# A post-norm decoder step on one core: the decode chain's tiles per step, its key products and the pace of its steps

## The chip, the cores and the metric

One core of a Trainium2 chip runs the whole program. The metric is the device time of one execution in microseconds, the median of the runs; lower is better. Engines are called as the profile calls them: PE (TensorE matmul), PEld (its weight load), DVE (VectorE), ACT (ScalarE), POOL (GpSimd), SP (SyncE, which here issues the prompt's DMAs).

## The reference, cut to what matters

One decoder layer is applied to two groups of requests that share all weights: a prompt of 1024 tokens, and eight requests that each decode one token against 4096 cached tokens.

```python
def trunk_layer(x, ...):                       # D_MODEL 1024, D_FF 2816, float32
    x = layer_norm(ALPHA * x + 0.5 * swiglu(x, f1_in, f1_out), ...)       # first half step
    h = x @ w_mix_in                                                       # q, k, v, u, vb: 5 x 512
    oa = diff_head_out(attend(q, k, v, lam), subln_g, lambda_init)         # 4 heads, 2 x 64 wide
    ob, vn = causal_sgu(u, vb, ...)
    x = layer_norm(ALPHA * x + concatenate([oa, ob]) @ w_mix_out, ...)
    x = layer_norm(ALPHA * x + cross_attn(x, mk, mv, xq_w, xo_w), ...)
    x = layer_norm(ALPHA * x + 0.5 * swiglu(x, f2_in, f2_out), ...)        # second half step

def sample_attend(ck, cv, page_table, table):  # the decode group's attend
    k_past = ck[page_table]; v_past = cv[page_table]      # 8 requests x 32 pages x 128 rows x 512
    ... softmax(q k_past / 8 + bias), two halves, p0 - lam * p1, times v_past
```

## The kernel before, in words

The prompt's work fills PE. Its matmuls have 344 (or 336) columns and come in threes, since each float32 operand is split into a high and a low part (`proj`, lines 150 to 152; the half step's `out`, lines 628 to 630). `ffn` walks eleven groups of two hidden blocks over three chunks of tokens; `unit` loads a block of weights by SP, and ACT and DVE split it (lines 63, 64). Line 635 adds a group's output to the accumulator on DVE. Then come `mix_first` and `mix_in` (projections of q, k, v and the gating unit), `attention`, `cross` and the second `ffn`.

The decode group's work is a generator, `decode`, which the prompt's loops advance. `beat(cols)` adds `rate[dstage] * cols / 8192` to a credit, and each whole credit runs one step of the chain (`step_dec`). So a rate is steps per 8192 matmul columns of the prompt, called a unit below. Stage 0 is the chain's own first half step and projection, stage 1 the key products, stage 2 the values. A scheduler in the compiler orders each engine's instructions by a timeline of its own; in stage 0, and in attention from its fifth step on, a step's instructions are held behind the PE matmul before it, in stage 1 behind a DVE instruction. In the other parts of stage 2 they can be moved earlier.

- **Stage 0** (`decode_keys`, lines 338 to 418, and `decode_sgu`): POOL loads one tile of weights a step into one of four buffers (`dec_stage`, line 332), and PE multiplies it by the eight tokens in four column groups of 32: 64 tiles of `w_in` (line 363), 32 of `w_out` (line 380), 24 of `w_mix_in` (line 406). Rate 2.6.
- **Stage 1** (lines 441 to 461): 17 tiles for each of eight requests; 16 of them are gathered from the paged cache by an indirect DMA on POOL (line 448), two rows of 512 a partition. DVE multiplies the tile by the query `qb` (line 453), and reduces the first row (line 454); ACT reduces the second row with eight accumulating copies (line 458). Lines 463 to 490 then make the softmax. Rate 1.0. When `ffn`'s last group begins, `before()` runs what is left (`dec_until(2)`).
- **Stage 2** (`decode_values`): one gathered tile a step (line 550), eight matmuls of one weight column on it (line 554). Its rate is 0 up to `mix_in`, there 0.9, 1.0, 4.0 and 0 for the four heads (line 835), and 2.0 in `attention` (line 1040). The scores `sc` lie in the pool of the four buffers; the pool `dv2` is opened in `before()` (line 1443).

From the code's own arithmetic, a group of `ffn` gives 18 units, `mix_first` 21, `mix_in` 43.5 and attention some 40. With the rates before, stage 0 ends in the third group, the key steps run to the tenth, `mix_in` issues 53 of the 128 value steps and attention 75.

Of the kernel before, what the change touches and what calls it, by code (L numbers as in the profile page):

```python
# [8 lines left out]
F32 = mybir.dt.float32  # L9
# [23 lines left out]
class Trunk:  # L33
    def __init__(self, ctx, tc, a, stop=None):
        self.ctx, self.tc, self.nc, self.a = ctx, tc, tc.nc, a
        self.stop = stop
        self.bg, self.free = [], []
        self.pinned = False
# [284 lines left out]
    def decode(self):  # L323
        with ExitStack() as ck:
            yield from self.decode_keys(self.pool("dk", 1, ck, side="right"))
        self.dstage = 2
        yield
        yield from self.decode_values()
        self.dstage = 3

    def dec_stage(self):
        return self.dv.tile([P, D], F32, tag="stg", bufs=4, name="stg")

    def decode_keys(self, dk):
# [19 lines left out]
        gT = dk.tile([P, 8, P], F32, name="gT")  # L354
        for s in range(4):
            ps = self.dec_bank()
            for half in range(2):
                c0 = half * D_FF + s * 704
                for k in range(KT):
                    st = self.dec_stage()  # L360
                    q.dma_start(st[:, :704], w_in[k * P:(k + 1) * P, c0:c0 + 704])
                    for j in range(4):
                        mm(ps[32 * j:32 * j + 32, half * 256:half * 256 + 176], xT[:, k], st[:, j * 176:(j + 1) * 176],
                           start=(k == 0), stop=(k == KT - 1))
                    yield
            t = dk.tile([P, 176], F32, tag="dt", bufs=1, name="dt")
            nc.scalar.activation(t, ps[:, :176], AF.Silu)
            nc.vector.tensor_tensor(t, t, ps[:, 256:432], op=ALU.mult)
            yield
            ps = self.dec_bank()  # L370
            for hh in range(2):
                nc.tensor.transpose(ps[:88, hh * P:(hh + 1) * P], t[:, hh * 88:(hh + 1) * 88], self.ident)
            nc.vector.tensor_copy(gT[:88, 2 * s:2 * s + 2], ps[:88, :256].rearrange("p (h i) -> p h i", h=2))
        ps = self.dec_bank()
        for n in range(32):
            s, j, hh = n // 8, n % 8 // 2, n % 2
            st = self.dec_stage()
            q.dma_start(st[:88], w_out[n * 88:(n + 1) * 88, :])
            for jj in range(4):
                mm(ps[32 * jj:32 * jj + 32, :256], gT[:88, 2 * s + hh, 32 * j:32 * j + 32],  # L380
                   st[:88, jj * 256:(jj + 1) * 256], start=(n == 0), stop=(n == 31))
            yield
# [15 lines left out]
        for g in range(3):  # L398
            ns = 2 if g < 2 else 1
            ps = self.dec_bank()  # L400
            for k in range(KT):
                st = self.dec_stage()
                q.dma_start(st[:, :512 * ns], w[k * P:(k + 1) * P, g * 1024:g * 1024 + 512 * ns])
                sv = st[:, :512 * ns].rearrange("p (s j c) -> p s j c", s=ns, j=4)
                for j in range(4):
                    mm(ps[32 * j:32 * j + 32, :P * ns], xT[:, k], sv[:, :, j], start=(k == 0), stop=(k == KT - 1))
# [11 lines left out]
        yield from self.decode_sgu(dk)  # L418

# [116 lines left out]
    def decode_values(self):  # L536
# [5 lines left out]
        for s in range(ND):  # L542
# [5 lines left out]
            for rr in range(16):  # L548
                st = self.dec_stage()
                q.indirect_dma_start(out=st, out_offset=None, in_=pages,  # L550
                                     in_offset=bass.IndirectOffsetOnAxis(ap=self.idx[:, s, rr:rr + 1], axis=0))
                for r in range(2):
                    for h in range(4):
                        mm(ps[32 * h:32 * h + 1, cs], self.sc[:, s, 2 * rr + r, 2 * h:2 * h + 1],  # L554
                           st[:, r * 512 + h * P:r * 512 + (h + 1) * P], start=(rr + r == 0), stop=False,
                           tile_position=(0, 32 * h))
                yield
# [239 lines left out]
    def mix_in(self, XH, XL, sl, tok):  # L797
# [36 lines left out]
        for h in range(4):  # L834
            self.rate[2] = (0.9, 1.0, 4.0, 0.0)[h]
# [77 lines left out]
    def attention(self, aq, at):  # L913
# [114 lines left out]
        for x in range(n + 4):  # L1028
# [9 lines left out]
            if x == 4:  # L1038
                self.pinned = True
                self.rate[2] = 2.0  # L1040
# [328 lines left out]
    def run(self):  # L1369
# [17 lines left out]
        self.sc = self.dv.tile([P, ND, 33, 8], F32, name="sc")  # L1387
        if self.stop == "dec":
            self.dec = self.decode()
            self.dec_until(2)  # L1390
            self.dv2 = self.pool("dv2", 1, cd, side="right", reuse_waits="tile")
# [7 lines left out]
        with ExitStack() as cx:  # L1399
# [5 lines left out]
            with ExitStack() as c1:  # L1405
# [35 lines left out]
                def before():  # L1441
                    self.dec_until(2)
                    self.dv2 = self.pool("dv2", 1, cd, side="right", reuse_waits="tile")
# [109 lines left out]
```

## Time and profile before

| | |
|---|---|
| median of 3 runs | 2597.42 us (2595.98 to 2598.25) |
| the profiled execution's own time | 2591.04 us |
| its span, first to last instruction | 2589.3 us |
| PE busy | 2476.6 us, 96% |
| DVE, ACT, POOL busy | 54%, 35%, 16% |
| mean granted clock of PE | 0.979 of full speed |

Busy PE is not PE at its peak: matmuls are pipelined, and one that waits for the one ahead counts as busy. What a stretch of PE's timeline costs is read from start to start. A granted clock below 1.00 in a stretch means that for part of it PE ran at the lower of its two levels, 1.2 instead of 2.4 GHz.

### The profile page before, as it was taken

The numbers are of one execution on the slowest core, as the hardware profiler recorded it, in microseconds if no ns is written. First come the engines' busy times: TensorE is split into PE (matmuls) and PEld (weight loads), VectorE is DVE, ScalarE is ACT, GpSimd is POOL, SyncE is SP. The second block draws the span as 40 slices with busy tenths as digits, with TensorE's granted clock in tenths as the row PEclk, the third lists the DMA queues.
The fourth block names the chain that finished last, engine by engine and source line by source line (L and its number), as shares of the span: only waits on it lengthen the run. The fifth ranks groups of instructions, "written<-read, shape, count | busy, mean of one in ns | idle before, by whom it ended". The sixth has DMA issues, their size and how long they took to land.

```text
span 2589.3 us, 45161 instructions
## 1 busy us (share of the span) xinstructions
PE 2476.6 (96%) x18032; PEld 2339.5 (90%) x18032; DVE 1387.4 (54%) x2706; ACT 908.5 (35%) x3334; POOL 422.3 (16%) x510
## 2 busy tenths in 40 slices
PE   8999999999999899898899999799999999999997
PEld 6777899999999799888677899789999999999997
DVE  4323388777778745614665473746633333333337
ACT  3111176666665341214655142533411111111110
POOL 2221243323332202120334000111000000000000
PEclk9999999999999899999999999999999999999999
DMA  6766566656654538778999732732211111111101
GB/s 214 233 199 185 188 200 203 187 181 194 192 184 142 198 124 267 249 238 260 272 301 311 248 110 96 231 108 75 66 50 49 49 42 47 43 50 49 50 17 66
DMA packets 294362, 399.28 MB, mean 154 GB/s; under 512 B 17132, under 2 KB 230948, under 8 KB 294152
## 3 DMA queue, kind: packets, MB, share of 16 engines
q0 software_dynamic: 57632, 205.00, 24.6%
q1 hardware_dynamic: 236520, 191.40, 24.4%
q8 instruction: 141, 2.31, 0.4%
q14 instruction: 69, 0.57, 0.1%
HBM read 352.68 MB, written 45.25 MB: 154 GB/s over the span
## 4 chain that ended last, share of the span: by engine, by line
PE 69%; DMA 9%; issue 6%; DVE 3%; ACT 1%; POOL 1%; SPq 0%; POOLq 0%; ACTq 0%; DVEq 0%
PE mm L150 16%; PE mm L151 16%; PE mm L152 16%; PE mm L628 5%; PE mm L629 5%; PE mm L630 5%; DMA stg<-cache_v,idx 4%; PE dec L554 1%; DMA raw<-xkv_w 1%; DMA stg<-cache_k,idx 1%; DVE stg L453 1%; DMA xqb<-xrows 1%; DMA qb<-rows 1%; PE dx L993 0%; DVE xst L1261 0%
## 5 line engine op out<-in xcount | busy, mean ns | idle before, releaser
L150 PE MATMUL mm<-XH,wh 128*128 128x344 f32 (+1 forms) x1536 | 497.8, 325 | 5.7 <-ACT XH L63 5.4
L152 PE MATMUL mm<-XH,wl 128*128 128x344 f32 (+1 forms) x1536 | 492.6, 321 | 0.0
L151 PE MATMUL mm<-XL,wh 128*128 128x344 f32 (+1 forms) x1536 | 492.3, 321 | 0.0
L63 ACT CAST wh<-raw 128x1024 fp32r<-128x1024 f32 x192 | 198.7, 1048 | 592.0 <-PE mm L629 274.6
L150 PE MATMUL mm<-YH,wh 128*128 128x344 f32 x1216 | 390.3, 321 | 6.0 <-ACT wh L63 6.0
L151 PE MATMUL mm<-YL,wh 128*128 128x344 f32 x1216 | 389.6, 320 | 0.0
L152 PE MATMUL mm<-YH,wl 128*128 128x344 f32 x1216 | 389.1, 320 | 0.0
L628 PE MATMUL mm<-gh,wh 128*128 128x344 f32 (+1 forms) x1040 | 336.3, 325 | 10.2 <-DVE g L611 5.0
L64 DVE TENSOR_TENSOR wl<-raw,wh 128x1024 fp32r<-128x1024 f32 x192 | 233.4, 1222 | 209.1 <-ACT wh L63 205.9
L629 PE MATMUL mm<-gl,wh 128*128 128x344 f32 (+1 forms) x1040 | 335.4, 323 | 0.0
L630 PE MATMUL mm<-gh,wl 128*128 128x344 f32 (+1 forms) x1040 | 334.6, 322 | 0.0
L150 PEld LDWEIGHTS mm<-XH,wh 128*128 128x128 f32 x1536 | 290.8, 190 | 18.2 <-issue 11.4
L152 PEld LDWEIGHTS mm<-XH,wl 128*128 128x128 f32 x1536 | 290.0, 189 | 5.5 <-issue 5.4
L151 PEld LDWEIGHTS mm<-XL,wh 128*128 128x128 f32 x1536 | 290.1, 189 | 4.9 <-issue 4.5
L458 ACT ACTIVATE stg<-stg 128x64 f32<-128x64 f32 x1024 | 246.7, 243 | 111.9 <-DVE stg L453 72.7
L611 DVE TENSOR_TENSOR g<-g,mm 128x344 f32<-128x344 f32 (+1 forms) x132 | 67.2, 509 | 347.7 <-PE mm L152 345.8
L150 PEld LDWEIGHTS mm<-YH,wh 128*128 128x128 f32 x1216 | 228.8, 188 | 8.6 <-ACT wh L63 6.8
L151 PEld LDWEIGHTS mm<-YL,wh 128*128 128x128 f32 x1216 | 228.9, 188 | 0.5 <-issue 0.4
L152 PEld LDWEIGHTS mm<-YH,wl 128*128 128x128 f32 x1216 | 228.7, 188 | 0.1
L628 PEld LDWEIGHTS mm<-gh,wh 128*128 128x128 f32 x1040 | 196.8, 190 | 19.6 <-issue 6.1
L550 POOL DMA_INDIRECT stg<-cache_v,idx x128 | 131.8, 1029 | 472.4 <-PE dec L554 429.9
L448 POOL DMA_INDIRECT stg<-cache_k,idx x128 | 157.5, 1230 | 284.1 <-DVE sc L454 119.4
(421 smaller groups left out, 4166.4 us busy)
## 6 DMA issues: line engine op xcount, KB each, us to landing
raw<-ffn_w_in SPq DMA_DIRECT2D x88, 512.0 KB
stg<-ffn_w_in POOLq DMA_DIRECT2D x64, 352.0 KB
raw<-ffn_w_out SPq DMA_DIRECT2D x44, 512.0 KB
stg<-ffn_w_out POOLq DMA_DIRECT2D x32, 352.0 KB
raw<-w_mix_in SPq DMA_DIRECT2D x20, 512.0 KB
stg<-w_mix_in POOLq DMA_DIRECT2D x16, 512.0 KB
raw<-xkv_w SPq DMA_DIRECT2D x16, 512.0 KB
xst<-cache_mem_k POOLq DMA_DIRECT2D x16, 512.0 KB
```

The costliest lines, as they stand in the source:

```text
L63: self.nc.scalar.copy(hi, src)
L64: self.nc.vector.tensor_tensor(lo, src, hi.bitcast(F32), op=ALU.subtract)
L150: mm(ps, wh[:, ks], xh[:, k], start=(i == 0), stop=False)
L151: mm(ps, wh[:, ks], xl[:, k], start=False, stop=False)
L152: self.pe_last = mm(ps, wl[:, ks], xh[:, k], start=False, stop=(i == KT - 1))
L448: q.indirect_dma_start(out=st, out_offset=None, in_=pages, in_offset=bass.IndirectOffsetOnAxis(ap=self.idx[:, s, rr:rr + 1], axis=0))
L458: nc.scalar.activation(v, v, AF.Copy, accum_out=sc[:, s, 2 * rr + 1, x:x + 1])
L550: q.indirect_dma_start(out=st, out_offset=None, in_=pages, in_offset=bass.IndirectOffsetOnAxis(ap=self.idx[:, s, rr:rr + 1], axis=0))
L611: self.anchor = nc.vector.tensor_tensor(g, g, pb, op=ALU.mult)
L628: nc.tensor.matmul(ps, wh[:, ds], gh, start=(i == 0), stop=False)
L629: nc.tensor.matmul(ps, wh[:, ds], gl, start=False, stop=False)
L630: self.pe_last = nc.tensor.matmul(ps, wl[:, ds], gh, start=False, stop=(i == len(fs) - 1))
```

## The change

Stage 0 collects four tiles and issues their matmuls in one step; its rate becomes 0.8 and its buffers seven (three more in the pool `dk`). The key stage gets pools of its own, so `sc` and the key buffers are allocated after stage 0. Of a key tile's product, DVE makes the first row and POOL the second; of the second row's reduction DVE takes four of the eight sums and ACT the other four; the query tile has two buffers; the rate becomes 1.3. A value step takes two tiles; its rate is 0.65 from the moment that the key stage ends, 0.4 in `mix_in` and 0.3 in attention. By the same arithmetic the key steps now end in the ninth group of `ffn`; the value tiles fall so: 50 in `ffn`, 28 in `mix_first`, 36 in `mix_in`, 14 in attention.

```diff
-        self.rate = [2.6, 1.0, 0.0, 0.0]
+        self.rate = [0.8, 1.3, 0.65, 0.0]
...
     def decode(self):
         with ExitStack() as ck:
-            yield from self.decode_keys(self.pool("dk", 1, ck, side="right"))
+            dk = self.pool("dk", 1, ck, side="right")
+            self.extra = [(dk, 3), (self.dv, 4)]
+            yield from self.decode_inputs(dk)
+            self.extra = []
+        self.sc = self.pool("dsc", 1, self.cd, side="right", reuse_waits="tile").tile([P, ND, 33, 8], F32, name="sc")
+        with ExitStack() as ck:
+            yield from self.decode_keys(self.pool("dk2", 1, ck, side="right", reuse_waits="tile"))
+        self.dv2 = self.pool("dv2", 1, self.cd, side="right", reuse_waits="tile")
         self.dstage = 2
...
     def dec_stage(self):
-        return self.dv.tile([P, D], F32, tag="stg", bufs=4, name="stg")
-
-    def decode_keys(self, dk):
+        pool, n = (self.dv, 4)
+        if self.extra:
+            self.staged = (self.staged + 1) % sum(n for _, n in self.extra)
+            pool, n = self.extra[0] if self.staged < self.extra[0][1] else self.extra[1]
+        return pool.tile([P, D], F32, tag="stg", bufs=n, name="stg")
+
+    def decode_inputs(self, dk):
...
                     q.dma_start(st[:, :704], w_in[k * P:(k + 1) * P, c0:c0 + 704])
-                    for j in range(4):
-                        mm(ps[32 * j:32 * j + 32, half * 256:half * 256 + 176], xT[:, k], st[:, j * 176:(j + 1) * 176],
-                           start=(k == 0), stop=(k == KT - 1))
+                    sts.append((half, k, st))
+                    if len(sts) < 4:
+                        continue
+                    for half, k, st in sts:
+                        for j in range(4):
+                            mm(ps[32 * j:32 * j + 32, half * 256:half * 256 + 176], xT[:, k],
+                               st[:, j * 176:(j + 1) * 176], start=(k == 0), stop=(k == KT - 1))
+                    sts = []
                     yield
...
-            qb = dk.tile([P, 512], F32, tag="qb", bufs=1, name="qb")
+            qb = dk.tile([P, 512], F32, tag="qb", bufs=2, name="qb")
...
-                nc.vector.tensor_tensor(sv, sv, qb.unsqueeze(1).to_broadcast([P, nr, 512]), op=ALU.mult)
+                nc.vector.tensor_tensor(sv[:, 0], sv[:, 0], qb, op=ALU.mult)
+                if nr == 2:
+                    q.tensor_tensor(sv[:, 1], sv[:, 1], qb, op=ALU.mult)
                 nc.vector.tensor_reduce(sc[:, s, 2 * rr], sv[:, 0].rearrange("p (x d) -> p x d", d=64), axis=AX.X, op=ALU.add)
                 if nr == 2:
-                    for x in range(8):
+                    nc.vector.tensor_reduce(sc[:, s, 2 * rr + 1, 4:], sv[:, 1, 256:].rearrange("p (x d) -> p x d", d=64),
+                                            axis=AX.X, op=ALU.add)
+                    for x in range(4):
...
-            for rr in range(16):
-                st = self.dec_stage()
...
+            for r0 in range(0, 16, 2):
+                sts = []
+                for rr in (r0, r0 + 1):
+                    st = self.dec_stage()
+                    q.indirect_dma_start(out=st, out_offset=None, in_=pages,
+                                         in_offset=bass.IndirectOffsetOnAxis(ap=self.idx[:, s, rr:rr + 1], axis=0))
+                    sts.append((rr, st))
+                for rr, st in sts:
...
-            self.rate[2] = (0.9, 1.0, 4.0, 0.0)[h]
+            self.rate[2] = 0.4
...
-                self.rate[2] = 2.0
+                self.rate[2] = 0.3
```

`w_out` and `w_mix_in` are collected by four in the same way. `dv2` is no longer opened in `before()`.

## Rows read from the trace of the kernel before

**Rows 1.** Busy time by stage: stretch, length, engines' busy us (instructions), granted clock, DMA share, GB/s
```profile
20.00:310.00 290.00, 282.96 (x2283) 226.08 (x2284) 93.86 (x188) 49.93 (x87) 67.60 (x126) 0.98 0.65 200
...
370.00:840.00 470.00, 468.05 (x2987) 466.55 (x2987) 378.88 (x551) 302.72 (x1933) 150.59 (x130) 1.00 0.60 185
...
985.00:1190.00 205.00, 193.04 (x1733) 181.91 (x1730) 91.23 (x182) 46.65 (x75) 41.12 (x45) 0.98 0.79 251
1190.00:1270.00 80.00, 64.40 (x583) 54.95 (x581) 42.77 (x113) 42.85 (x122) 15.80 (x17) 0.91 1.03 295
1270.00:1446.00 176.00, 164.00 (x1908) 133.36 (x1908) 101.29 (x306) 93.47 (x285) 64.15 (x70) 0.97 0.92 293
```
**Rows 2.** Timeline of PE, weight steps alone and four together: start, us, engine, line
```profile
103.95 0.32 PE L630 MATMUL mm<-gh,wl 128*128 128x344 f32 x1
104.20 0.51 PE L363 MATMUL dec<-stg,xT 128*32 128x176 f32 x8
104.64 0.42 PE L628 MATMUL mm<-gh,wh 128*128 128x344 f32 x1
...
113.37 1.40 PE L363 MATMUL dec<-stg,xT 128*32 128x176 f32 x32
114.70 0.42 PE L629 MATMUL mm<-gl,wh 128*128 128x344 f32 x1
```
**Rows 3.** Busy time of VectorE's product line L453 alone in the key stage
```profile
370.00:840.00 470.00, 140.32 (x121) 1.00 0.60 185
```
**Rows 4.** Busy time of VectorE's reduction line L454 alone in the key stage
```profile
370.00:840.00 470.00, 79.24 (x121) 1.00 0.60 185
```
**Rows 5.** Groups of VectorE by line and shape, 330 to 815 us
```profile
L453 DVE TENSOR_TENSOR stg<-stg,qb 128x1024 f32<-128x1024 f32 x126 | 151.6, 1220 | 39.3 <-DMA stg<-cache_k,idx 23.7 <-DMA qb<-rows 14.2 <-issue 1.3
...
L453 DVE TENSOR_TENSOR stg<-stg,qb 128x512 f32<-128x512 f32 x8 | 5.5, 687 | 0.0
```
**Rows 6.** Timeline of POOL and of VectorE in the key stage
```profile
503.33 0.93 POOL L448 DMA_INDIRECT stg<-cache_k,idx  x1 [6.00 <-DVE g L611]
509.68 1.59 POOL L448 DMA_INDIRECT stg<-cache_k,idx  x1 [5.41 <-DVE A L635]
...
509.24 1.22 DVE L453 TENSOR_TENSOR stg<-stg,qb 128x1024 f32<-128x1024 f32 x1
```
**Rows 7.** Groups of POOL by line: one with data of 128 elements a partition
```profile
L723 POOL TENSOR_SCALAR_AFFINE_SELECT sgw<-sgw 128x128 f32<-128x128 f32 x4 | 1.0, 312 | 0.0
```
**Rows 8.** Timeline of PE, value steps alone and two together
```profile
1146.10 0.62 PE L554 MATMUL dec<-stg,sc 128*1 128x128 f32 x16
1146.64 0.43 PE L152 MATMUL mm<-XH,wl 128*128 128x336 f32 x1
...
1136.80 1.06 PE L554 MATMUL dec<-stg,sc 128*1 128x128 f32 x32
1137.78 0.42 PE L151 MATMUL mm<-XL,wh 128*128 128x344 f32 x1
```
**Rows 9.** Busy time of the value line L554 alone, by stretch
```profile
840.00:900.00 60.00, 12.88 (x240) 5.76 (x240) 0.89 0.60 200
...
985.00:1190.00 205.00, 21.03 (x592) 13.63 (x592) 0.98 0.79 251
1190.00:1446.00 256.00, 48.26 (x1200) 24.52 (x1200) 0.95 0.96 294
```
**Rows 10.** Chain of waits in attention, 1190 to 1446 us, by line
```profile
by line: DMA stg<-cache_v,idx 25.1%; DMA raw<-xkv_w 13.6%; PE dec L554 8.1%; issue 6.4%; PE dx L993 5.0%; PE mm L150 4.9%; PE mm L151 4.9%; PE mm L152 4.7%; DMA q<-scr_qh 4.2%; PE f L985 3.4%; PE s L955 3.4%; PE s L960 2.6%; DMA kh<-scr_kh 
```
**Rows 11.** A wait of PE in attention: us in total, times, longest
```profile
PE dec L554 <- DMA stg<-cache_v,idx: 9.1, 9, 3.7
```
**Rows 12.** Chain of waits behind attention: start us, us, what
```profile
1450.24 2.14 DMA OLs<-dol
1452.61 1.05 ACT wh L63
1453.70 0.65 PE mm L150
```

More of the change, by code (lines that the diff above doesn't have):

```diff
@@ L37, in __init__ @@
         self.bg, self.free = [], []
+        self.extra, self.staged = [], 0
         self.pinned = False
         self.dec, self.dstage, self.credit, self.anchor, self.pe_last = None, 0, 0.0, None, None
-        self.rate = [2.6, 1.0, 0.0, 0.0]
+        self.rate = [0.8, 1.3, 0.65, 0.0]
         self.cst = self.pool("cst", 1)
@@ L378, in decode_keys @@
             q.dma_start(st[:88], w_out[n * 88:(n + 1) * 88, :])
-            for jj in range(4):
-                mm(ps[32 * jj:32 * jj + 32, :256], gT[:88, 2 * s + hh, 32 * j:32 * j + 32],
-                   st[:88, jj * 256:(jj + 1) * 256], start=(n == 0), stop=(n == 31))
+            sts.append((n, gT[:88, 2 * s + hh, 32 * j:32 * j + 32], st))
+            if len(sts) < 4:
+                continue
+            for n, g, st in sts:
+                for jj in range(4):
+                    mm(ps[32 * jj:32 * jj + 32, :256], g, st[:88, jj * 256:(jj + 1) * 256], start=(n == 0), stop=(n == 31))
+            sts = []
             yield
@@ L403, in decode_keys @@
                 q.dma_start(st[:, :512 * ns], w[k * P:(k + 1) * P, g * 1024:g * 1024 + 512 * ns])
-                sv = st[:, :512 * ns].rearrange("p (s j c) -> p s j c", s=ns, j=4)
-                for j in range(4):
-                    mm(ps[32 * j:32 * j + 32, :P * ns], xT[:, k], sv[:, :, j], start=(k == 0), stop=(k == KT - 1))
+                sts.append((k, st[:, :512 * ns].rearrange("p (s j c) -> p s j c", s=ns, j=4)))
+                if len(sts) < 4:
+                    continue
+                for k, sv in sts:
+                    for j in range(4):
+                        mm(ps[32 * j:32 * j + 32, :P * ns], xT[:, k], sv[:, :, j], start=(k == 0), stop=(k == KT - 1))
+                sts = []
                 yield
@@ L418, in decode_keys @@
         yield from self.decode_sgu(dk)
+    def decode_keys(self, dk):
+        nc, a = self.nc, self.a
+        mm = nc.tensor.matmul
+        q = nc.gpsimd
         pt = dk.tile([P, ND], I32, name="pt")
@@ L547, in decode_values @@
             q.dma_start(vn, self.rows[2, s:s + 1, :])
-            for rr in range(16):
-                st = self.dec_stage()
[L550 to L556, printed above, removed]
+            for r0 in range(0, 16, 2):
+                sts = []
+                for rr in (r0, r0 + 1):
[4 more added lines that the diff above has]
+                for rr, st in sts:
+                    for r in range(2):
+                        for h in range(4):
+                            mm(ps[32 * h:32 * h + 1, cs], self.sc[:, s, 2 * rr + r, 2 * h:2 * h + 1],
+                               st[:, r * 512 + h * P:r * 512 + (h + 1) * P], start=(rr + r == 0), stop=False,
+                               tile_position=(0, 32 * h))
                 yield
@@ L1386, in run @@
         self.dv = self.pool("dv", 1, cd, side="right")
-        self.sc = self.dv.tile([P, ND, 33, 8], F32, name="sc")
+        self.cd = cd
         if self.stop == "dec":
@@ L1390, in run @@
             self.dec_until(2)
-            self.dv2 = self.pool("dv2", 1, cd, side="right", reuse_waits="tile")
             self.dec_until(3)
@@ L1442, in before @@
                     self.dec_until(2)
-                    self.dv2 = self.pool("dv2", 1, cd, side="right", reuse_waits="tile")
                     lnp.append(self.pool("lnp", 1, c1, side="right", reuse_waits="tile"))
```

## The prediction

> **What bounds the kernel now.** I read the busy times by stage first [rows 1]. In the key stage, 370 to 840 us, PE is dense: 468 of 470 us, clock 1.00, and 2987 matmuls give 0.157 us each from start to start. A unit of 8192 columns is 24 such matmuls, about 3.8 us. DVE is busy 379 of the 470 us there, so PE is the bound and DVE stands close behind. Around it PE is not dense. In stage 0 it also carries the chain's small matmuls. In attention it is idle for 15.6 us of the 80 up to 1270 us and for 12.0 of the 176 behind, at granted clocks of 0.91 and 0.97 (what is missing there is time at 1.2 GHz), while the DMA engines are full (shares of 1.03 and 0.92). The chain of waits in attention names the value tiles' loads first, 25.1% of 256 us [rows 10], and PE itself waited 9.1 us for such tiles [rows 11]. So the chain costs twice: as small matmuls between the large ones, and as loads that attention waits for.
>
> **The change, part by part.** *Stage 0.* A w_in step alone takes PE from the 103.95 us matmul to the 104.64 us one: 0.69 us, less the 0.16 of the large matmul, so 0.53. Four steps that the scheduler happened to put together take 1.33 us from their own start to the next large matmul, with the same lead-in of 0.25 us, less 0.16: 1.42 [rows 2]. So each border between the two kinds of matmul costs (4 x 0.53 - 1.42) / 3 = 0.23 us, whatever lies between. I counted the timeline's runs: 96 for the 120 tiles, two of which stand in the rows. The change makes 30. 66 borders at 0.23 give **-15 us**, all on PE's path. What it adds: the fourth tile of a step can load only when the step before has given its buffers back, and four DMAs then stand behind one another on POOL, which is busy for 68 of 290 us there [rows 1], so its queue has room. A step comes every 1.25 units, 4.7 us and its own 1.4. No row shows a late tile's price; the bounds are no wait at all and 0.5 us in each of the 30 steps, 15 us, which would give the gain back. I take no wait, since the DMA share is 0.65.
>
> *Query tile.* DVE sat idle 14.2 us for eight query loads [rows 5]; PE felt little of it, being within 2 us of dense [rows 1]. A second buffer takes **-2**; bounds 0 and -5.
>
> *Key stage.* A tile costs DVE 140.32 / 121 = 1.16 us for the product [rows 3] and 79.24 / 121 = 0.65 for the reduction [rows 4]; the other 159 us of its 379, over some 124 units, are the prompt's, 1.29 us a unit. At 1.3 tiles a unit a tile has 2.92 us, of which 0.99 are the prompt's. The product of one row is 687/1220 of the whole [rows 5], 0.65; the reduction stays 0.65; half a row more is by the same ratio 0.37. Together 2.66 of 2.92: **0.26 us a tile to spare**. POOL gets a product that no row shows. Its nearest rows are DVE's 0.69 us for the same data [rows 5] and POOL's 0.312 us for a quarter of the elements with one input [rows 7], times four 1.25; I take 1.0. With 0.93 to 1.59 us for a gather [rows 6] POOL then has 1.9 to 2.6 us of work in 2.92. On POOL the product waits for its tile, and later gathers queue behind it; four buffers leave room for three of them. DVE's added reduction waits for POOL's product, with the prompt's weight splits queued behind it, and PE waits for those.
>
> The row at 509.68 us shows what the two engines do to each other: a gather that takes 0.93 us beside no product takes 1.59 beside DVE's product of 509.24, ending 0.8 us behind it, while that product keeps its 1.22 us [rows 6]. So POOL gave way. Whether DVE gives way to a POOL product no row shows: the bounds are 0 and the whole product, 1.25 us a tile. I take 0.36, a third of 1.0 as the chance to meet, and little more: 0.10 beyond the spare for 136 tiles, **+14 us**. The Trainium skill (SBUF — State Buffer, section Who interferes with whom) speaks against this edit: a DVE instruction with two SBUF inputs and a GpSimd instruction that reads SBUF take a shared read interface, and the later one waits for the whole of the other. The trace agrees as far as the gather that stretched to 1.59 us. The skill (GPSIMD Engine Reference, section 3.1 Elementwise) also gives 4497 ns for a two-input operation on 2048 elements, by estimate 1.1 us here; by that price and the same third the term would be +19 instead of +14.
>
> ACT loses four of its eight copies a tile; nothing waits for ACT there, so that is nothing. The softmax of the scores moves from the last group of the half step into the ninth; it is DVE work among dense PE either way: nothing, with 0 to -5 for the norm behind the half step, which then starts on a freer DVE.
>
> *Values.* A step alone costs 0.25 + 0.54 - 0.16 = 0.63 us of PE, two together 0.25 + 0.98 - 0.16 = 1.07 [rows 8]. 64 pairs for 128 steps: 68.5 instead of 80.6, -12. Some stand together already (+3). And 240 of the records, 15 steps, lie in the norm's hole at 840 to 900 us, 12.9 us [rows 9], where PE has nothing else; a hole now filled only by half gives back some 5. Left: **-4**. This holds the moves: of 75 steps in attention 14 tiles stay, the other 61 cost the half step and the projections 61 x 0.54 = 33 us and attention gets back 61 x 0.64 = 39 [rows 9].
>
> *What attention waits for.* Idle time 27.6 us; at clocks of 0.91 and 0.97 the lower level fills some 25 us, of which half, 12, is lost [rows 1]: 40 in all. 61 of 75 tiles leave, and their loads are the first name on the chain [rows 10]; other names (xkv_w 13.6%, q 4.2%) waited in part because of them. I take 60%, **-24**; bounds 0 and -40. Late next is xkv_w.
>
> *The chain's tail.* Behind attention PE stood until 1453.70 us for ACT's split of 1452.61, which waited for the chain's last DMA [rows 12]. The tail now runs inside attention: **-8**, the 6 us hole and some of the slower matmuls behind it; bounds -5 and -10.
>
> *Loads in new places.* Tiles now fall on `mix_first`, the end of `mix_in` and the first 80 us of attention, where the share is 1.03 already [rows 1]: **+2**; bounds 0 and 12.
>
> Sum: -15 - 2 + 14 - 4 - 24 - 8 + 2 = **-37**. Against the profiled execution's 2591.0 us: 2554. That execution is 6.4 us below the median of the runs, so the median goes to **2560 us**.
>
> **The rivals.** *DVE becomes the bound in the key stage (slower).* Place: the fourth to the ninth group of the half step, 136 tiles. Each POOL product holds DVE up for w; beyond 0.26 us PE stands for 136 x (w - 0.26). The other terms give -51, so the sign turns at w = 0.26 + 51/136 = 0.64 us. At w = 0.9, nearly every product meeting one of DVE's, +87: 2560 - 14 + 87 = 2633. For: both products start when the same tile lands, and DVE has 9% to spare. Against: in the rows POOL gave way [rows 6], and the five banks of psA let PE run ahead of DVE. The lock that would do it is the one of the Trainium skill's page SBUF — State Buffer, cited above.
>
> *Attention's holes were free.* If half of the 39 us of value matmuls lay where PE had nothing else, moving them frees 20 less, and the waits shrink by 14 rather than 24: 2590. For: idle time stands there beside them [rows 1]. Against: the chain names loads, not softmax work.
>
> *Attention was bound by loads throughout.* All 40 us go, the key stage gives nothing, and of the 12 us in which PE is idle at 985 to 1190 us [rows 1] 8 go too, since the burst of 36 steps there is gone: 2560 - 16 - 14 - 8 = 2522.
>
> *The steps don't stay together.* The scheduler made runs of four of its own and moved 15 value steps out of `mix_in` to 840 us. If it splits the new steps or their fourth tile is late, -15 and -4 go: 2579.
>
> **How the numbers follow.** Forecast 0.45, DVE as bound 0.14, free holes 0.13, loads throughout 0.23, split steps 0.05. The range reaches from below the loads case, 2515, to past the free holes, 2606, and leaves most of the DVE case out; the bounds of the other terms (15 for late tiles, 12 for new places) lie inside. A difference of 0.2%, 5 us, is what a measurement of this kernel can tell. Faster: 0.45 + 0.23 + about half of 0.13 + nearly all of 0.05 = 0.79. Slower: 0.14. Same: 0.07.
>
> **What would show it.** In the changed profile: w_in runs of 32 records throughout and the key stage starting some 15 us sooner; PE still dense at the key stage, with DVE near 90% busy and its product no longer than 0.7 us; value runs of 32 records; attention some 65 us shorter (39, 24 and a little), clock nearer 1.00; no wait for `OLs<-dol` behind it. Waits of PE for L635 or for split weights in the key stage, or DVE products of over 1 us, would prove the first rival; a half step longer by more than some 55 us would make the forecast wrong.

## The result and the profile after

The changed kernel takes 2682.3 us, median of four runs (2674.7 to 2693.4), against 2596.7 for the kernel before: a ratio of 1.033, 95% interval 1.030 to 1.037. It is slower by 86 us where 37 us of gain were forecast, and 76 us above the range's upper end. The profiled execution took 2674.7 us (span 2673.0) at a mean granted clock of 0.964.

Where the time went is seen best by a mark that both kernels share: the end of each of the half step's eleven groups, read as the last accumulation on DVE of the group (L635 before, L674 after). Worked out from the traces, in us, for the two kernels and for the experiments below; "behind" is from there to the end of the span:

```
kernel                      groups 1-3   4   5    6    7    8    9   10   11  behind  span
before                         315      77   65   68   69   69   67   68   73  1718   2589
after                          313      77   88   89   83   86   87   82   85  1684   2673
f3  before, pace 1.3           317      79   75   76   74   74   68   66   73  1732   2635
e1  after, product on DVE      309      73   76   80   74   73   74   83   85  1692   2621
e3  e1 + POOL memset           313      76   79   81   78   76   75   82   85  1698   2643
e2  e1 + POOL product          314      79   84   86   86   85   77   84   85  1699   2678
g3  e1, six buffers            310      82   71   68   68   66   71   83   85  1707   2611
h1  after, six buffers         310      87   94   84   74   82   89   82   85  1704   2691
f1  before, fours              313      73   70   66   67   67   68   67   73  1730   2595
```

The key stage fills groups 5 to 9 after the change: 433 us for what took 338, **+95**. The last two groups carry the first value tiles, +26. Stage 0 gained 2, and everything behind the half step 34. (That last part moves between executions: before, f1 and f3 run the same work there and differ by 14.) The experiments split the +95 (differences taken before rounding): with DVE making the whole product (e1) groups 5 to 9 are 40 longer than before, with six buffers as well (g3) 6. So POOL's product is worth 55 of the 95, and too few buffers at the new pace 34.

The busy times of the kernel after by stage (stretch, length, PE, PEld, DVE, ACT, POOL, granted clock, DMA share, GB/s):

```profile
20.00:312.00 292.00, 275.46 (x2326) 243.09 (x2325) 99.02 (x206) 54.54 (x93) 65.40 (x124) 0.97 0.65 197
370.00:820.00 450.00, 387.48 (x2265) 375.01 (x2264) 406.10 (x612) 180.81 (x1033) 310.00 (x251) 0.90 0.60 184
...
1320.00:1388.00 68.00, 50.11 (x377) 43.03 (x376) 41.74 (x111) 37.16 (x111) 5.63 (x6) 0.85 1.02 281
1388.00:1564.00 176.00, 156.35 (x1163) 140.81 (x1162) 107.85 (x325) 95.52 (x292) 10.08 (x14) 0.96 0.60 176
```

Against [rows 1] the second row is the result: PE was dense in the key stage, 468 of 470 us at clock 1.00, and is now busy 387 of 450 at 0.90, while DVE is at 90%. The waits of PE in 330 to 780 us name DVE (us in total, times, longest):

```profile
PE mm L667 <- DVE g L650: 36.0, 11, 6.4
PE mm L667 <- DVE A L674: 11.7, 9, 2.0
PE mm L667 <- ACT g L649: 7.3, 5, 3.1
```

55 us in 25 waits; before, PE waited there once for `g`, 5.0 us, and three times for the accumulation, 2.0 us in all. DVE's groups there, shapes apart (busy, mean ns, idle time before and its releaser):

```profile
L484 DVE TENSOR_TENSOR stg<-stg,qb 128x512 f32<-128x512 f32 x132 | 153.5, 1163 | 31.0 <-DMA stg<-cache_k,idx 30.5
L487 DVE TENSOR_REDUCE sc<-stg 128x8 f32<-128x512 f32 x131 | 88.1, 675 | 0.5
L489 DVE TENSOR_REDUCE sc<-stg 128x4 f32<-128x256 f32 x124 | 50.4, 407 | 8.6 <-POOL stg L486 8.6
L65 DVE TENSOR_TENSOR wl<-raw,wh 128x1024 fp32r<-128x1024 f32 x32 | 48.4, 1513 | 3.0 <-ACT wh L64 3.0
L674 DVE TENSOR_TENSOR A<-A,mm 128x344 f32<-128x344 f32 x80 | 38.3, 498 | 0.0
L65 DVE TENSOR_TENSOR gl<-g,gh 128x344 fp32r<-128x344 f32 x21 | 19.9, 950 | 0.0
```

The first of these rows is the one to learn to doubt. Half a product took 687 ns before [rows 5]; it now takes 1163, so that 132 half products cost DVE as much (153.5 us) as 126 whole ones did (151.6, [rows 5]). Its work was halved and its time was not. The splits of the prompt's operands (`wl`, `gl`) are longer too, 1513 and 950 ns where they take 1215 and 507 in the run e1 below; the reductions (one SBUF operand) and the accumulation (one operand from SBUF, one from PSUM) are what they were. POOL's product in the same stretch:

```profile
L486 POOL TENSOR_TENSOR stg<-stg,qb 128x512 f32<-128x512 f32 x125 | 177.4, 1423 | 58.4 <-DMA stg<-cache_k,idx 50.9 <-DVE A L674 3.7 <-ACT stg L493 1.2
```

A mean hides what happens to one product. All 136 of DVE's (shortest, median and longest in ns), and the longest of them beside POOL (start, us):

```profile
L484 DVE TENSOR_TENSOR stg<-stg,qb x136: 672/717/4546, 337.2 to 787.0; 128x512 f32<-128x512 f32 x136
...
344.27 4.55 DVE L484 TENSOR_TENSOR stg<-stg,qb 128x512 f32<-128x512 f32 x1
...
343.07 1.38 POOL L479 DMA_INDIRECT stg<-cache_k,idx  x1 [2.38 <-ACT gh L64]
344.46 3.79 POOL L486 TENSOR_TENSOR stg<-stg,qb 128x512 f32<-128x512 f32 x3
```

Half of the products keep some 0.7 us; counted in the timeline, 66 are stretched (over 0.8 us), to 1.66 on average. The longest begins 0.19 us before three products of POOL in a row and ends with the last of them. To begin first is thus no protection: of the 39 that did so, 23 kept 0.7 us while POOL's product took up to 1.80 instead, but 16 were held for the whole of POOL's product. In all 16, POOL was just issuing a gather when DVE began.

One long wait of PE, read in the timelines of DVE, POOL and PE (start, us):

```profile
440.63 1.44 DVE L484 TENSOR_TENSOR stg<-stg,qb 128x512 f32<-128x512 f32 x1
441.99 1.26 DVE L487 TENSOR_REDUCE sc<-stg 128x8 f32<-128x512 f32 x2
443.18 0.40 DVE L489 TENSOR_REDUCE sc<-stg 128x4 f32<-128x256 f32 x1
443.51 1.21 DVE L65 TENSOR_TENSOR wl<-raw,wh 128x1024 fp32r<-128x1024 f32 x1
444.64 0.68 DVE L484 TENSOR_TENSOR stg<-stg,qb 128x512 f32<-128x512 f32 x1
445.24 1.93 DVE L496 TENSOR_TENSOR sc<-sc,bd 128x264 f32<-128x264 f32 x1
447.10 0.50 DVE L650 TENSOR_TENSOR g<-g,mm 128x344 f32<-128x344 f32 x1
...
440.02 1.50 POOL L486 TENSOR_TENSOR stg<-stg,qb 128x512 f32<-128x512 f32 x1
...
445.60 1.28 POOL L486 TENSOR_TENSOR stg<-stg,qb 128x512 f32<-128x512 f32 x1
...
435.63 0.42 PE L667 MATMUL mm<-gh,wh 128*128 128x336 f32 x1 [2.99 <-DVE g L650]
...
436.36 0.48 PE L668 MATMUL mm<-gl,wh 128*128 128x336 f32 x1
436.64 0.48 PE L669 MATMUL mm<-gh,wl 128*128 128x336 f32 x1
440.24 0.65 PE L667 MATMUL mm<-gh,wh 128*128 128x336 f32 x1 [3.12 <-ACT g L649]
...
447.65 0.65 PE L667 MATMUL mm<-gh,wh 128*128 128x336 f32 x1 [5.36 <-DVE g L650]
```

DVE is never idle from 440.63 on. The product of 440.63 starts beside POOL's product of 440.02 to 441.52 and takes 1.44 us; that of 444.64 meets none and takes 0.68. The addition of 445.24 (L496) takes 1.93 us beside POOL's product of 445.60, and 0.42 to 0.43 us for the other requests. PE's next operand, `g` of 447.10, stands in order behind all of it, and PE waits 5.36 us. PE also pays a second time: from 436.36 us on its matmuls follow each other every 0.28 us, not every 0.157. The clock granted in that stretch, from windows of the same trace:

```profile
440.00:447.60 7.60, 2.05 (x6) 1.62 (x6) 7.60 (x11) 3.12 (x11) 6.95 (x7) 0.50 0.73 210
447.60:451.00 3.40, 3.35 (x12) 3.30 (x12) 3.40 (x4) 2.51 (x17) 1.77 (x3) 0.50 0.99 356
```

0.50 is the lower level, 1.2 GHz. PE did not fall to it by the wait of 5.36 us: it had stood for 2.99 us up to 435.63, ran four matmuls, fell at 436.36, and stayed low through the waits of 3.12 and 5.36 us until 456.7. In 370 to 820 us 171 of the 2258 large matmuls are followed at 0.22 to 0.33 us; at 0.157 they would take 21 us less. So of the 95 us lost some 21 are clock.

### The profile page after: what moved, and what is told of

Same layout as the page of the kernel before. It is cut to its first block, busy times and chain, and to the rows that moved or that the text cites. A ratio compares the mean times of both kernels' runs of the same rounds, so it can differ in the third digit from the quotient of the medians.

```text
span 2673.0 us, 44425 instructions
## 1 busy us (share of the span) xinstructions
PE 2490.2 (93%) x18032; PEld 2372.0 (89%) x18032; DVE 1444.2 (54%) x2834; ACT 786.4 (29%) x2310; POOL 585.5 (22%) x638
## 3 DMA queue, kind: packets, MB, share of 16 engines
q0 software_dynamic: 57632, 205.00, 24.1%
## 5 line engine op out<-in xcount | busy, mean ns | idle before, releaser
L667 PE MATMUL mm<-gh,wh 128*128 128x344 f32 (+1 forms) x1040 | 350.8, 339 | 64.5 <-DVE g L650 44.1
L65 DVE TENSOR_TENSOR wl<-raw,wh 128x1024 fp32r<-128x1024 f32 x192 | 242.8, 1271 | 202.3 <-ACT wh L64 199.7
L668 PE MATMUL mm<-gl,wh 128*128 128x344 f32 (+1 forms) x1040 | 344.6, 331 | 1.2 <-DVE gl L65 1.2
L669 PE MATMUL mm<-gh,wl 128*128 128x344 f32 (+1 forms) x1040 | 343.4, 330 | 0.0
L667 PEld LDWEIGHTS mm<-gh,wh 128*128 128x128 f32 x1040 | 204.9, 197 | 82.3 <-DVE g L650 48.9
L587 POOL DMA_INDIRECT stg<-cache_v,idx x128 | 125.8, 983 | 466.6 <-PE dec L593 440.0
L668 PEld LDWEIGHTS mm<-gl,wh 128*128 128x128 f32 x1040 | 206.1, 198 | 1.8 <-DVE gl L65 1.6
L669 PEld LDWEIGHTS mm<-gh,wl 128*128 128x128 f32 x1040 | 205.5, 198 | 0.6 <-issue 0.6
```

The source lines that it names most:

```text
L65: self.nc.vector.tensor_tensor(lo, src, hi.bitcast(F32), op=ALU.subtract)
L587: q.indirect_dma_start(out=st, out_offset=None, in_=pages, in_offset=bass.IndirectOffsetOnAxis(ap=self.idx[:, s, rr:rr + 1], axis=0))
L667: nc.tensor.matmul(ps, wh[:, ds], gh, start=(i == 0), stop=False)
L668: nc.tensor.matmul(ps, wh[:, ds], gl, start=False, stop=False)
L669: self.pe_last = nc.tensor.matmul(ps, wl[:, ds], gh, start=False, stop=(i == len(fs) - 1))
```

## The experiments

Differences in us are between the median of a kernel and that of the kernel before measured beside it; intervals are those of the ratio.

**e1: the product back on DVE.** The second row's reduction is back on ACT alone, too. Everything else is the change, its pace of 1.3 included.

```diff
-                nc.vector.tensor_tensor(sv[:, 0], sv[:, 0], qb, op=ALU.mult)
-                if nr == 2:
-                    q.tensor_tensor(sv[:, 1], sv[:, 1], qb, op=ALU.mult)
+                nc.vector.tensor_tensor(sv, sv, qb.unsqueeze(1).to_broadcast([P, nr, 512]), op=ALU.mult)
...
-                    for x in range(4):
+                    for x in range(8):
```

> The changed kernel with the key arithmetic of before (DVE makes the whole product, ACT the eight sums of the second row) at the new pace of 1.3. Theory lock (POOL's product and DVE's instructions with two SBUF inputs hold each other up): the key stage is dense on PE again, DVE's product 1.22 us for a whole tile and weight splits 1.22 us, time 2590 to 2615 us, some 75 below the changed kernel's 2682. Theory pace (1.3 tiles a unit overload DVE whoever multiplies: 1.16 + 0.65 + 0.99 = 2.80 of 2.92 us): PE still stands for DVE in the key stage, 2650 us or more. Theory queue (the product keeps POOL from issuing gathers): as lock.

2626.7 us, +30.0 (1.0136, 1.009 to 1.018), between the two theories' times. POOL's product, with DVE's part of the second row's reduction, costs 56 us of the 86; 30 are something else.

**e2 and e3: POOL busy with work that nobody waits for.** e1, and after each DVE product a POOL instruction on a scratch tile: a product of 128x512 (e2), or a memset of 128x1024 (e3).

```diff
+                if nr == 2:
+                    q.tensor_tensor(own[:, 1], own[:, 0], own[:, 0], op=ALU.mult)     # e2
+                    q.memset(own, 0.0)                                                # e3
```

> The kernel of e1_dve_product, with one POOL product of 128x512 a tile on buffers of its own, which nobody waits for. Theory lock: the weight splits go back to some 1.4 us and the whole-tile product to 1.5 us or more, PE stands in the key stage, 2660 to 2700 us. Theory data (DVE stood because it waited for POOL's result): as e1_dve_product, within 10 us. Theory queue: 2650 us or more, but the splits keep their 1.22 us.

> The kernel of e1_dve_product, with one POOL memset of 128x1024 a tile on a buffer of its own, some 1.2 us, which reads no SBUF and which nobody waits for. Theory lock by reads: as e1_dve_product within 10 us, splits 1.22 us. Theory queue: as e2_idle_pool_product, since POOL is held as long. If the splits grow here too, the lock isn't one of reads alone.

e2: 2675.9 us, +79.2 (1.0308, 1.027 to 1.035). e3: 2649.9, +53.2 (1.0213, 1.018 to 1.025). DVE's product and split in 330 to 720 us, first e1, then e2, then e3:

```profile
L484 DVE TENSOR_TENSOR stg<-stg,qb 128x1024 f32<-128x1024 f32 x125 | 152.1, 1220 | 42.4 <-DMA stg<-cache_k,idx 39.4 <-ACT stg L489 2.6
...
L65 DVE TENSOR_TENSOR wl<-raw,wh 128x1024 fp32r<-128x1024 f32 x31 | 37.5, 1215 | 0.3 <-ACT wh L64 0.3
...
L65 DVE TENSOR_TENSOR gl<-g,gh 128x344 fp32r<-128x344 f32 x21 | 10.6, 507 | 0.0
```

```profile
L486 DVE TENSOR_TENSOR stg<-stg,qb 128x1024 f32<-128x1024 f32 x108 | 174.0, 1614 | 16.8 <-DMA stg<-cache_k,idx 16.7
L489 DVE TENSOR_REDUCE sc<-stg 128x8 f32<-128x512 f32 x112 | 75.0, 675 | 0.4
L65 DVE TENSOR_TENSOR wl<-raw,wh 128x1024 fp32r<-128x1024 f32 x28 | 44.4, 1584 | 3.1 <-ACT wh L64 3.1
```

```profile
L485 DVE TENSOR_TENSOR stg<-stg,qb 128x1024 f32<-128x1024 f32 x119 | 144.9, 1220 | 51.7 <-DMA stg<-cache_k,idx 49.5 <-ACT stg L492 1.9
...
L65 DVE TENSOR_TENSOR wl<-raw,wh 128x1024 fp32r<-128x1024 f32 x30 | 36.3, 1215 | 2.7 <-ACT wh L64 2.7
```

No other engine uses the result of POOL's scratch product, and still DVE's products (1614) and splits (1584 ns) are longer by 0.4 us each; beside the memset, which keeps POOL nearly as long (0.97 us against 1.19), they are unchanged. So it is not data and not POOL being busy that lengthens them: a POOL operation that reads SBUF holds up a DVE operation with two SBUF inputs, and a reduction, with one, is spared (675). That is the rule of the Trainium skill (SBUF — State Buffer, section Who interferes with whom), which the forecast had cited and priced too low; here the trace bears it out, the exemption of writes included. That the later one waits, as the forecast also had from there, holds only in part: 16 products of the change were held though they had begun first (above). The memset's own 23 us, without any stretched instruction on DVE, are not explained by the rule. In the traces some 14 of them lie in groups 4 to 9, and DVE waited 49.5 us for tiles there against 39.4 in e1: gathers that come late behind the memset would fit, but no run shows it.

**e4: the change at pace 1.0.**

```diff
-        self.rate = [0.8, 1.3, 0.65, 0.0]
+        self.rate = [0.8, 1.0, 0.65, 0.0]
```

> The changed kernel with POOL's product, at the old pace of 1.0 in the key stage. Theory lock: each tile has 3.8 us instead of 2.92, the product stays near 1.1 us for half a tile, PE stands less but still does, 2610 to 2650 us. Theory pace: as dense as before, 2570 to 2600 us.

2664.2 us, +67.5 (1.0258, 1.021 to 1.030): both theories missed. By the same marks its groups 5 to 9 take 373 us, 60 less than the change's and still 35 more than before; but what is behind the half step takes 1736, 52 more than the change's. The slower key steps leave value tiles over: the last is used at 1513.7 us, 72 us behind the start of attention's last scores, where in the change it is 34 us ahead of it. What the run shows is the stretch at the old pace: products 904 ns and splits 1433, milder than in the change, and still there.

**f1 to f4: each part alone, on the kernel before.** f1 has stage 0 in fours with seven buffers and its rate 0.8. f2 has two value tiles a step, at half the old rates. f3 has the key pace 1.3, with the product on DVE as before. f4 has the values from the half step's last group on.

```diff
-        self.rate = [2.6, 1.0, 0.0, 0.0]
+        self.rate = [2.6, 1.3, 0.0, 0.0]      # f3
+        self.rate = [2.6, 1.0, 1.3, 0.0]      # f4, and 0.8 in mix_in, 1.3 in attention
```

> The kernel before with the new stage 0 alone: four tiles a step at 0.8, seven buffers; key products, values and their rates are those of before. Theory borders (66 fewer borders on PE at 0.23 us): 2575 to 2585 us, keys starting some 10 us sooner than at 316 us. Theory burst (six tiles loaded at once delay the prompt's first loads, and each step's fourth tile comes late): the first w_in matmul at some 40 instead of 24 us, w_out runs over 2.5 us long, keys starting at 322 us or later, 2600 to 2612 us.

> The kernel before with value steps of two tiles at half the rates (0.45, 0.5, 2.0, 0 and 1.0), so the tiles fall in the same places. Theory borders: PE spends some 10 us less on values, 2582 to 2594 us. Theory late loads (a pair waits for its second tile, with four buffers only one pair ahead): the runs get holes inside, 2597 us or more.

> The kernel before with the key rate at 1.3 instead of 1.0, DVE still making the whole product, values as before. Theory pace (DVE has 2.80 of 2.92 us to do, and waits for tiles in it block the prompt's splits): PE stands 20 to 40 us in the key stage, and nothing uses the time won behind it, 2610 to 2635 us. If the pace is harmless without POOL's product: 2590 to 2600 us.

> The kernel before with the value steps, one tile each, spread at 1.3 from the half step's last group on, 0.8 in mix_in and 1.3 in attention: 86 of the 128 tiles are issued ahead of attention instead of 53. Theory loads (attention waits for value tiles; moved out of it they free 20 us or more): 2570 to 2585 us. Theory free holes (the value matmuls lay where PE had nothing else): 2592 to 2610 us.

f1: 2590.3, -6.1 (0.9969, 0.995 to 0.999). f2: 2588.8, -7.6 (0.9973, 0.996 to 0.999). f3: 2642.6, **+46.2** (1.0178, 1.015 to 1.020). f4: 2603.4, +7.0 (1.0029, 1.001 to 1.005). f1 missed both of its theories' times, and f3 lies above the one that it bears out. Both regroupings are a little faster, but f2 not by fewer borders: in its trace the value tiles stand in 106 runs, before in 105, so hardly a pair stayed together, and PE waited 15.5 us for such tiles against 9.1. What its 7.6 us come from is open. The pace alone, without POOL's product, costs more than the whole gain that was forecast; 29 of its 46 us lie in groups 5 to 9. And taking 33 value tiles out of attention gains nothing, which speaks against the term for attention's waits. How the pace stops PE, in f3's timelines of DVE, POOL and PE:

```profile
440.51 0.51 DVE L64 TENSOR_TENSOR gl<-g,gh 128x344 fp32r<-128x344 f32 x1
442.11 1.23 DVE L453 TENSOR_TENSOR stg<-stg,qb 128x1024 f32<-128x1024 f32 x1 [1.09 <-DMA stg<-cache_k,idx]
443.25 0.51 DVE L611 TENSOR_TENSOR g<-g,mm 128x344 f32<-128x344 f32 x1
...
434.72 1.19 POOL L448 DMA_INDIRECT stg<-cache_k,idx  x1 [5.35 <-ACT stg L458]
436.87 1.18 POOL L448 DMA_INDIRECT stg<-cache_k,idx  x1 [0.97 <-ACT stg L458]
...
443.81 0.65 PE L628 MATMUL mm<-gh,wh 128*128 128x336 f32 x1 [3.72 <-DVE g L611]
```

DVE is idle for 1.09 us, since the product at the head of its queue waits for a tile, and the prompt's `g`, ready to go, stands behind it; PE waits 3.72 us for that. The tile is late because the buffers were: its gather, that of 436.87, stood in POOL's order behind one that had waited 5.35 us for ACT's sums of an earlier tile, and then waited 0.97 us itself. (f3 has one query buffer, and DVE's waits for queries, 12.7 us at 330 to 700 us, are in its time too; e1, with two, has none.)

**g3 and g4: late tiles or an occupied DVE?** g3 is e1 with two more key buffers, six in all. g4 is e1 without the second row's product, so that DVE has 0.5 us a tile less.

```diff
+        self.extra, self.staged = [(dk, 2), (self.dv, 4)], 0      # g3, in the key stage
...
-                nc.vector.tensor_tensor(sv, sv, qb.unsqueeze(1).to_broadcast([P, nr, 512]), op=ALU.mult)
+                nc.vector.tensor_tensor(sv[:, 0], sv[:, 0], qb, op=ALU.mult)      # g4
```

> The changed kernel with the whole product on DVE (2626.7 us, pace 1.3) and two more buffers for key tiles, six in all. Theory of late tiles: at pace 1.3 the DVE product waits for a gather and the prompt's weight splits stand behind it; with two more tiles on the way that ends, PE's excess over its pace in the key stage falls to about 13 us and the time to 2590 to 2605. Theory of an occupied DVE: the waits are of DVE's own work, the buffers change nothing, 2620 to 2632.

> The changed kernel with the whole product on DVE, but the second row's product is left out altogether (ACT sums the row as it was loaded, so these scores are other numbers): DVE has 0.5 us a tile less, 68 us in all, POOL nothing more. Theory of an occupied DVE: PE stands no more, the time falls by 25 to 40 us to 2587 to 2602. Theory of late tiles: the gathers come when they came, 2615 to 2630.

g3: 2609.6, +11.3 (1.0052, 1.003 to 1.007). g4: 2623.5, +25.2 (1.0116, 1.008 to 1.015). Busy times in 370 to 700 us, of e1, of g3 and of g4:

```profile
370.00:700.00 330.00, 305.19 (x1883) 296.99 (x1882) 291.60 (x416) 250.35 (x1741) 138.40 (x119) 0.97 0.70 218
```

```profile
370.00:700.00 330.00, 323.11 (x2030) 319.32 (x2030) 309.20 (x442) 263.87 (x1841) 187.86 (x124) 0.99 0.74 237
```

```profile
370.00:700.00 330.00, 317.95 (x1979) 312.53 (x1979) 243.77 (x424) 252.45 (x1777) 120.33 (x118) 0.98 0.71 224
```

With six buffers DVE is *busier* than in e1 (309 of 330 us against 292) and PE denser (323 against 305, clock 0.99). With the shorter product DVE is idle a quarter of the time and PE stands more than in g3. So at this pace tiles are late, and DVE's occupation matters less: the buffers give back 19 us, the shorter product 5 at most. g3's time is some 5 us above what the theory of late tiles had; in the table its groups 5 to 9 are 66 to 71 us, 6 in all above before, and group 4, where the key stage starts, is 5 above.

**h1 to h3: is POOL's product late tiles too?** The change, e2 and e3, each with the six buffers of g3 (h2 and h3 with one query buffer, for want of room).

> The changed kernel itself with six key buffers instead of four. Late-tile theory of the POOL product (it delays the gathers behind it on POOL, nothing else): 2615 to 2630, within 20 us of the run with the product on DVE and six buffers (2609.6). Lock theory (DVE's products and the prompt's splits are held up themselves): splits stay at 1.5 us, and at most the 17 us of late tiles come back, 2655 to 2675.

> Whole product on DVE, POOL makes a product of the same size on a scratch tile that nobody reads, six key buffers (one query buffer, for want of room). With four buffers 2675.9. Late-tile theory: 2615 to 2630. Lock theory: splits stay at 1.5 us, 2645 to 2665.

> As the run above, with a memset of 128x1024 on POOL in place of the product, six key buffers, one query buffer. With four buffers 2649.9, 23 over the run without it. If those 23 us are gathers that come late behind the memset in POOL's queue, two more tiles on the way take them away: 2609 to 2620. If the memset takes something else from the other engines, 2630 to 2640.

h1: 2687.9, +88.6 (1.0337, 1.030 to 1.037). h2: 2666.7, +67.4 (1.0259, 1.022 to 1.030). h3: 2637.9, +38.6 (1.0149, 1.011 to 1.019). h1 and h2 come out above the times that the lock theory gave. The change itself gains nothing from more buffers, where its twin on DVE gained 19. h1's groups of DVE, 330 to 720 us:

```profile
L486 DVE TENSOR_TENSOR stg<-stg,qb 128x512 f32<-128x512 f32 x117 | 151.5, 1296 | 7.1 <-DMA stg<-cache_k,idx 7.1
...
L65 DVE TENSOR_TENSOR wl<-raw,wh 128x1024 fp32r<-128x1024 f32 x27 | 48.4, 1793 | 1.5 <-ACT wh L64 1.5
```

The tiles come in time (7.1 us of waiting, 24.1 in the change in the same stretch). The two engines don't meet more often, 57 of 136 products are stretched against 66, but a stretched one takes 2.08 us against 1.66, and up to 4.88, the longest where several of POOL's products follow one another: 1296 ns on average for the half product, 1793 for the split. That is the lock again, and with late tiles gone it is not cheaper: h1 stands 77 us above g3. Between the idle product and the idle memset it is 26 us with four buffers and 29 with six. The memset's own cost stays, 23 and 27 us; late gathers behind it in POOL's queue were to vanish with more buffers and did not, but h3 has one query buffer, for which DVE waited 22.0 us, so its cause is left open.

**g1, g2 and h4: the parts that gain, together.** g1 is fours, pairs and two query buffers, with the key stage before. g2 ties the fifth load to the first step's buffer. h4 is g1 with six key buffers.

> The first half step's fours and the value pairs of the change, with the key stage's product on DVE alone, its pace of 1.0 and the values' old places (pairs at half the rates), and two query buffers. If the two gains seen alone (6.4 and 7.9 us) add up, 2580 to 2585 us, a ratio of 0.9945. If they were one and the same slack (the norm's hole and attention's waits taking up what stage 0 gives), 2588 to 2592, no better than either alone.

> The kernel above, with the fifth tile's load bound to the buffer of the first step, so that only four tiles are loaded while the prompt comes in, as before. If the chain's late first step (42 instead of 24 us) is what the fours pay for, the stage ends some 12 us sooner and the time falls by 5 to 12 us, to 2570 to 2578. If that time is only moved (PE has other matmuls of the prompt to do and the chain's place does not matter), no change, within 3 us of the kernel above.

> Fours and pairs with the key stage at pace 1.0 on DVE (2591.0), and six key buffers. If tiles are late now and then at the old pace too (PE's excess over its pace there is 13 us, and 8 to 11 us wait on DVE's accumulations), 2583 to 2588. If the old pace leaves the gathers time enough, no change, 2589 to 2593.

g1: 2591.0, -7.3 (0.9975, 0.9956 to 0.9995). g2: 2591.0, -7.3 (0.9981, 0.996 to 1.000). h4: 2589.4, -9.9 (0.9966, 0.995 to 0.998). The two gains do not add: together they are what either is alone. In g1 and h4, too, the pairs did not stay together (109 and 104 runs of value tiles, 105 before), so nothing was saved there to add. g2 settles nothing, since its trace shows POOL issuing six tile loads in one run from 2.5 us on, as the change does: the compiler moved the loads ahead, and the start was not held. h4 lies within g1's interval. These versions and f1 and f2 are 0.2 to 0.3% faster than the kernel before, g2's interval reaching 1.000.

## Why the prediction was wrong

The step that failed is the **key stage**, +14 in the sum and +95 in the groups. It had two parts, the price of POOL's product and the spare time that was to carry it, and both fell.

*The price of the lock.* I took w = 0.36 us a tile, "a third of 1.0 as the chance to meet", and a little more. The price of a meeting was right: a stretched product is longer by 0.98 us. The chance was not, 66 of 136, half and not a third, and the splits, which are held up as well, were left out. In means: the half product is longer by 1163 - 687 = 0.48, and 32 splits of each kind add 32 x (0.30 + 0.31) / 132 = 0.15 a tile (`gl` over both of its shapes 0.82 against 0.51). So w = 0.63. By my own formula that is 136 x (0.63 - 0.26) = +50, just at the first rival's turning point of 0.64; between e1 and the change groups 5 to 9 differ by 55. I read the chance as random; but both halves start when the same tile lands, which I had written down in favour of that rival and then not used. The row of 509.68, in which POOL gave way, was one case of two: 16 products show the other. POOL's product, taken as 1.0 us with 1.25 as the bound, is 1.42 beside DVE, outside the bound, and 1.19 on the scratch tile of e2. The figure of the Trainium skill (GPSIMD Engine Reference, section 3.1 Elementwise), 1.12 by estimate, is nearer than mine and still under both.

*The spare of 0.26 us a tile.* It was an average: DVE's work per tile against the time per tile. f3 has no POOL product and by this reckoning (1.16 + 0.65 + 0.99 = 2.80 of 2.92) should have been free; it costs 46 us, and e1's groups 5 to 9 are 40 longer than before. An engine that runs in order has no spare time to share out: what counts is whether the instruction at its head can start. At 1.3 tiles a unit four buffers are too few, the product waits, and the prompt's work waits with it. g3 shows that cause, with 34 of these 40 back, and g4 that it is not in the main the load on DVE. The sum had no term for tiles that come late at the new pace.

The other terms:

- *Stage 0, -15.* f1 gave -6.1. The trace has 38 runs, not 30, and the price of 0.23 us a border held roughly: groups 2 to 4 are shorter by 12 in g1 (260 against 272 us). Group 1 is longer by 7. Some steps were split where the fourth tile was late, the bound I had named and put at zero, as here in the kernel after:

```profile
82.96 1.10 PE L380 MATMUL dec<-stg,xT 128*32 128x176 f32 x24
...
89.27 0.51 PE L380 MATMUL dec<-stg,xT 128*32 128x176 f32 x8 [2.66 <-DMA stg<-ffn_w_in]
```

- *Values, -4.* f2 gave -7.6, but its pairs fell apart (106 runs), so the agreement of sign is luck and shows nothing of the borders. In the change itself there are 74 runs, not 64; what they saved was not tried alone. The moved tiles cost the last two groups 26 us where 50 x 0.54 = 27 were reckoned.
- *Attention's waits, -24.* Nothing of it came. From the first score matmul to the last transpose of an output (L1008 before, L1047 after) attention takes 212 us (1320.5 to 1532.7) after and 224 (1201.8 to 1425.8) before, 12 less, where 39 for the moved matmuls and 24 for the waits were forecast. In the profile after, DMA shares fell from 0.92 to 0.60 in the second part, and PE is idle 17.9 + 19.6 = 37.5 us, not less than the 27.6 of before; the clock fell from 0.91 and 0.97 to 0.85 and 0.96. Instead of value tiles, PE's waits in 1320 to 1564 us name:

```profile
PE dx L919 <- DVE mkr L921: 9.3, 2, 7.1
PE s L994 <- ACT p L1007: 8.3, 10, 1.7
PE dx L919 <- ACT o L1034: 4.9, 1, 4.9
```

  This is the second rival, "attention's holes were free": the chain of waits named the loads because they ended last, not because nothing stood just behind them. The trace before had the sign of it, one row above that of [rows 11], in PE's waits at 1190 to 1446 us, and the prediction did not read it:

```profile
PE s L955 <- ACT p L968: 9.3, 5, 4.3
```

  PE waited longer for the softmax than for value tiles. The third rival, loads throughout, does not fit these rows nor f4. "Late next is xkv_w" was wrong too; it is the softmax and the transposes of the memory keys.
- *Tail, -8.* PE's wait of 6.0 us for ACT's split behind attention is gone from the list; right in kind.
- *Query tile, -2, and loads in new places, +2.* Not tried alone; g1, with two query buffers, is no better than f1.

Of the signs named as proof of the first rival two came: PE waits for the accumulation (L674; 11.7 us) and products over 1 us on average. PE's waits for split weights did not come; it waited for `g`. And waits for the accumulation prove less than I had thought: e1, without POOL's product, has them too (9.3 us at 330 to 720 us). DVE at 90%, which also came, had been named as a sign of the forecast. The half step is longer by 118 us (989 against 871), over the 55 that were to make the forecast wrong.

## What to carry to other kernels

Halving DVE's product by sharing it with POOL was worth nothing here, since both halves read SBUF at the same moment; price such a pair as one after the other, and count the other operations on DVE with two SBUF inputs as well. For an engine that works in order, compare not its mean load with the pace but the time from a buffer's release to its next tile: raise the number of buffers before the pace. And a wait that ends last on the chain is worth only its lead over the next one.

## What the runs showed of the hardware that was not expected

A DVE product that has begun is not safe from POOL: at 344.27 us one was held for three POOL products in a row, 4.55 us instead of 0.7, though it had begun first. That happened in the change only where POOL was issuing a gather as DVE began; a gather alone lengthens no product of the kernel before (at most 1.23 us for a whole one). Why the two together do so is open.

A POOL memset that shares no data with DVE and lengthens none of its instructions costs 23 us over some 130 of 0.97 us each; late gathers behind it would fit, but its cause was not shown.

And a wait of PE can be paid twice: in f3, after 3.72 us of standing, the matmuls of 443.81 us and after run at one every 0.28 us; in the change the clock fell after a wait of 2.99 us and four matmuls, and stayed at 0.50 for some 20 us.
